# Three kinds of small elementwise work of a recurrent mixer moved from VectorE to GpSimd

## Chip, cores and metric

The kernel runs on one core of one Trainium2 chip. The metric is the device time of one execution in microseconds (us), as the median of three runs. The engines are named as in the profile: PE is TensorE, DVE is VectorE, ACT is ScalarE, POOL is GpSimd, SP is SyncE, which issues the transfers.

## What is computed

Two sequences of 512 tokens, each of width 1024, go through a trunk of two layers. Each layer projects the tokens, runs two token mixers beside each other, merges them with gates and ends with a squared-ReLU MLP. The mixer that matters here is a bidirectional gated linear recurrence with eight heads of 64 keys and 64 values:

```python
def step(S, inp):
    qc, kc, vc, gc = inp
    b = jnp.cumsum(gc, axis=2)
    diff = b[:, :, :, None, :] - b[:, :, None, :, :]
    dec = jnp.exp(jnp.where(tri[:, :, None], diff, -jnp.inf))
    A = jnp.einsum('bhtd,bhsd,bhtsd->bhts', qc, kc, dec)
    o = jnp.einsum('bhts,bhse->bhte', A, vc) + jnp.einsum('bhtd,bhde->bhte', qc * jnp.exp(b), S)
    ...
k_f, g_f = gates(hf_fwd, lower[0])
k_b, g_b = gates(hf_bwd, lower[1])
o_f = gla_chunk_scan(q, k_f, v, g_f)
o_b = rev(gla_chunk_scan(rev(q), rev(k_b), rev(v), rev(g_b)))
o = o_f + o_b
```

## The kernel before

Both sequences (the kernel calls them groups, g = 0 and 1) pass each layer together. All large products are done in three passes of rounded halves (`mm3`, L152 to L154, tile `mm`), and each weight block that comes in is split into such halves: ACT casts it (L131) and POOL, or in some places DVE, subtracts (L132, tile `w`).

The recurrent mixer is `hgrn`. It handles two heads at a time, so it has four passes p = 0 to 3 for each layer. The decay is not computed as a table of differences; the block of scores is built up over levels of distance h = 1, 2, 4 and so on to 64. At each level `grow` multiplies queries Q (L418) and keys K (L422) by products of the gates, and `tot` (L428) holds those products. For h = 2 to 64 the two heads' queries are laid out in a block-diagonal tile `bd`: `spread` copies the first head's 64 partitions with ACT (L348) and the second head's with DVE (L346). PE then multiplies (`quads`, L355, or L399 in `far`), and DVE writes the results into `near` under a mask (`keep`, L363). At level h = 32 (`middle`) the four 32-row quarters of `near` are copied into the score tile `at` (L390), beside the products of that level, which DVE and ACT take from PSUM in turn (L386). At h = 64 (`far`) ACT copies the results (L406).

The distance-one neighbours are done apart, in `pairs`, once for each pass and group. A straight product `ox` and a crosswise product `other` (L253: queries of even places by keys of odd ones and the other way round, two instructions of 128x256) are each split into halves (ACT L258, DVE L259), summed over a head's channels by PE (L261 and L262, each pair into one bank `sm`), and multiplied by the values (DVE L264 for `ox`, L267 for `other`); POOL adds the two (L270).

While PE runs pass p's levels, the projections of pass p + 1 (`prep`, whose instructions fill PE between the levels) run between them: `weave` takes one step of each in turn. In the last pass the gates' projections take their place. Pass 0's `prep` runs alone, ahead of everything, in each layer.

What sets the order: every engine runs its own instructions strictly in the order in which the program's scheduler put them, and waits at semaphores for the others. The scheduler places instructions by its own estimates, so a change of engine for some of them can also change the order of others. `pool_copy` (L134 and L135) is a helper that copies on POOL, as a multiplication by 1.0; before, it is used once, for the first weight block.

Of the kernel before, what the change touches and what calls it, by code (L numbers as in the profile page):

```python
# [87 lines left out]
def tile_encoder_trunk(  # L88
# [6 lines left out]
    nc = tc.nc  # L95
# [16 lines left out]
    def sm_ps():  # L112
        return psum.tile([P, 512], F32, tag="sm", name="sm")
# [20 lines left out]
    def pool_copy(dst, src):  # L134
        nc.gpsimd.tensor_scalar(dst, src, 1.0, None, op0=ALU.mult)  # L135
# [94 lines left out]
    def hgrn(l, x, gate):  # L230
        with tc.tile_pool(name=f"hg{l}", bufs=1) as hp:
# [14 lines left out]
            def t2k(dt=F32):  # L246
                return hp.tile([P, SEQ], dt, tag="t2k", name="t2k", bufs=4)

            def pairs(r, vt):
                ox = r["ox"]  # L250
                other = t2k()
                for i in range(2):
                    nc.vector.tensor_tensor(  # L253
                        other[:, i::2], r["q"][:, i, i::2], r["k"][:, 1 - i, 1 - i::2], op=ALU.mult
                    )
                hi, lo = t2k(F32R), t2k(F32R)
                for w in (ox, other):
                    nc.scalar.copy(hi, w)  # L258
                    nc.vector.tensor_tensor(lo, w, hi.bitcast(F32), op=ALU.subtract)  # L259
                    ps = sm_ps()  # L260
                    nc.tensor.matmul(ps, ones, hi, start=True, stop=False)  # L261
                    nc.tensor.matmul(ps, ones, lo, start=False, stop=True)  # L262
                    if w is ox:
                        nc.vector.scalar_tensor_tensor(ox, ps, 64.0, vt, op0=ALU.mult, op1=ALU.mult)  # L264
                        continue
                    for i in range(2):
                        nc.vector.scalar_tensor_tensor(  # L267
                            w[:, i::2], ps[:, i::2], 64.0, vt[:, 1 - i::2], op0=ALU.mult, op1=ALU.mult
                        )
                    nc.gpsimd.tensor_tensor(ox, ox, w, op=ALU.add)  # L270

            def prep(p, u):
                for col in (C_FF, C_FB, C_HQ, C_HI, C_HG):
# [7 lines left out]
                    for g in (range(NG), (1, 0))[l > 0 and p == 0]:  # L281
# [28 lines left out]
                        elif col == C_HI:  # L310
                            vt = t2k()
                            nc.scalar.copy(vt, ps)
                            ps = sm_ps()
                            for c in range(4):
                                s = slice(c * P, (c + 1) * P)
                                nc.tensor.transpose(ps[:, s], vt[:, s], ident)
                            v = hp.tile([P, 4, P], F32, tag="V", name="V", bufs=2)
                            nc.scalar.copy(v, ps)
                            r["v"] = v
                            pairs(r, vt)  # L320
                        else:
                            sg = t2k()
                            nc.scalar.activation(out=sg, in_=ps, func=AF.Sigmoid)
                            hg = hp.tile([P, SEQ], F32, tag="hg", name="hg", bufs=2)
                            nc.vector.tensor_tensor(hg, ps, sg, op=ALU.mult)
                            r["hg"] = hg
# [7 lines left out]
            def queries(r, h):  # L334
                return bass.AP(
                    r["q"].tensor, r["q"].offset, [list(r["q"].ap[0]), [2 * h, SEQ // (2 * h)], [SEQ + h, 2], [1, h]]
                )

            def spread(g, src):
                for e in range(2):  # L340
                    hs = slice(64 * e, 64 * e + 64)
                    dst = bd[g][hs, e, :]
                    if len(src.shape) == 4:
                        dst = dst.rearrange("p (n x h) -> p n x h", x=2, h=src.shape[3])
                    if e:
                        nc.vector.tensor_copy(dst, src[hs])  # L346
                    else:
                        nc.scalar.copy(dst, src[hs])  # L348

            def quads(g, lhs, swap):  # L350
                ps = sm_ps()
                for c in range(4):
                    for i in range(4):
                        o = c * P + 32 * (i ^ swap)
                        nc.tensor.matmul(  # L355
                            ps[32 * i:32 * i + 32, c * 64:(c + 1) * 64].rearrange("p (e t) -> p e t", e=2),
                            lhs(c, i), bd[g][:, :, o:o + 32], start=True, stop=True,
                            tile_position=(0, 32 * i),
                        )
                return ps  # L360
# [8 lines left out]
            def short(g, r, n, h):  # L369
                spread(g, queries(r, h))  # L370
                kx = hp.tile([P, SEQ], F32, tag="kx", name="kx", bufs=2)
                nc.scalar.copy(kx.rearrange("p (n x h) -> p n x h", x=2, h=h), keys(r, h))
                ps = quads(g, lambda c, i: kx[:, c * P + 32 * i:c * P + 32 * i + 32], 0)
                keep(g, ps, n)

            def middle(g, r):
                spread(g, queries(r, 32))
                ps = quads(
                    g, lambda c, i: r["k"][:, i % 2, c * P + 32 * i:c * P + 32 * i + 32], 1
                )  # L380
                A, N = at[g], near[g]
                for i in range(4):
                    hs = slice(32 * i, 32 * i + 32)
                    o = 32 * (i ^ 1)
                    eng = nc.scalar.copy if i % 2 else nc.vector.tensor_copy
                    eng(  # L386
                        A[hs, :, :, o:o + 32].rearrange("p c e t -> p (c e) t"),
                        ps[hs, :256].rearrange("p (c t) -> p c t", t=32),
                    )
                    nc.vector.tensor_copy(A[hs, :, :, hs], N[hs])  # L390

            def far(g, r):
                spread(g, queries(r, 64))
# [382 lines left out]
    for l in range(DEPTH):  # L776
# [9 lines left out]
        for k in (4, 5, 6, 7, 0, 1, 2, 3):  # L786
            raw = raw_tile()
            nc.sync.dma_start(raw, o_sp[l][k])
            for g in range(NG):
                src = raw[:, g * SEQ:(g + 1) * SEQ]  # L790
# [292 lines left out]
```

## Time and profile before

| | |
|---|---|
| median of three runs | 3065.37 us (3060.91 to 3068.12) |
| profiled execution, its own time | 3064.09 us |
| its span, first to last instruction | 3062.3 us |
| PE busy | 2956.7 us, 97% of the span |
| DVE busy | 1666.7 us, 54% |
| ACT busy | 1090.9 us, 36% |
| POOL busy | 865.8 us, 28% |
| the two recurrent mixers, in us of the span | about 55 to 395 and 1590 to 1910 |

Busy time is the time in which an engine ran an instruction. The chain of work that ended last goes through PE for 81% of the span and through DVE for 10%. A row of a timeline gives start, duration, engine, line, operation, tile written and tiles read, shapes and count, and in brackets how long the engine had stood idle and what ended that. A row of instructions of the same kind that follow each other has one start and one duration for all of them.

### The profile page before, as it was taken

How to read it: one execution, taken by the hardware profiler on the slowest of the kernel's cores; microseconds unless marked ns; L12 is line 12 of the kernel's file. 1: busy time of each engine (PE TensorE's matmuls, PEld its weight loads, DVE VectorE, ACT ScalarE, POOL GpSimd, SP SyncE). 2: the span in 40 equal slices, each digit the busy share in tenths (PEclk: the TensorE clock that was granted, in tenths of full speed). 3: DMA queues.
4: the chain of work that ended last, by engine and by line, in shares of the span. 5: the costliest groups of instructions: out<-in, count | busy, mean ns of one | idle time of the engine just before them, and what ended most of it. 6: DMA issues, size and time to landing. Idle time of an engine off the chain costs nothing.

```text
span 3062.3 us, 42748 instructions
## 1 busy us (share of the span) xinstructions
PE 2956.7 (97%) x16720; PEld 2399.4 (78%) x16720; DVE 1666.7 (54%) x2877; ACT 1090.9 (36%) x1826; POOL 865.8 (28%) x532
## 2 busy tenths in 40 slices
PE   8999999999999999999889999999999999999997
PEld 6777787877888887888667777878878888878885
DVE  5888748126543333445768887481265433344448
ACT  3344447323121112433434444473231211124333
POOL 4222120112222222454542221101231222234544
PEclk9999999999999999999999999999999999999999
DMA  3111232246123346533321112322460243564333
GB/s 127 36 42 36 67 89 69 80 162 218 34 86 134 132 167 241 169 97 97 113 75 36 42 36 69 90 64 100 157 226 9 93 144 125 177 255 144 97 97 107
DMA packets 278890, 331.98 MB, mean 108 GB/s; under 512 B 16545, under 2 KB 185121, under 8 KB 274593
## 3 DMA queue, kind: packets, MB, share of 16 engines
q1 hardware_dynamic: 276816, 325.00, 32.5%
q10 hardware_dynamic: 1872, 4.26, 0.4%
q8 instruction: 131, 2.15, 0.3%
q14 instruction: 71, 0.57, 0.1%
HBM read 230.38 MB, written 92.27 MB: 105 GB/s over the span
## 4 chain that ended last, share of the span: by engine, by line
PE 81%; DVE 10%; DMA 3%; issue 3%; POOL 1%; ACT 1%; SPq 0%; ACTq 0%; POOLq 0%; DVEq 0%
PE mm L152 17%; PE mm L154 16%; PE mm L153 16%; PE sm L971 3%; PE sm L972 3%; PE sm L973 3%; PE mm L972 3%; PE mm L971 3%; PE mm L973 3%; PE mm L864 2%; PE mm L866 2%; PE mm L865 2%; PE sm L695 1%; PE sm L641 1%; PE sm L685 1%
## 5 line engine op out<-in xcount | busy, mean ns | idle before, releaser
L152 PE MATMUL mm<-X,w 128*128 128x512 f32 x2624 | 1033.4, 394 | 4.8 <-ACT w L131 4.1
L153 PE MATMUL mm<-X,w 128*128 128x512 f32 x2624 | 1028.7, 392 | 0.0
L154 PE MATMUL mm<-X,w 128*128 128x512 f32 x2624 | 1026.2, 391 | 1.1 <-POOL w L132 1.1
L132 POOL TENSOR_TENSOR w<-raw,w 128x1024 fp32r<-128x1024 f32 (+1 forms) x179 | 417.9, 2336 | 1370.9 <-ACT w L131 1255.2
L152 PEld LDWEIGHTS mm<-X,w 128*128 128x128 f32 x2624 | 493.6, 188 | 111.8 <-ACT w L131 4.5
L154 PEld LDWEIGHTS mm<-X,w 128*128 128x128 f32 x2624 | 493.8, 188 | 102.3 <-POOL w L132 2.2
L153 PEld LDWEIGHTS mm<-X,w 128*128 128x128 f32 x2624 | 493.8, 188 | 98.6 <-DVE X L793 0.5
L131 ACT CAST w<-raw 128x1024 fp32r<-128x1024 f32 (+1 forms) x330 | 332.1, 1007 | 365.4 <-PE sm L973 106.7
L902 DVE TENSOR_TENSOR X<-t 128x512 f32<-128x512 f32 x128 | 88.6, 692 | 427.8 <-ACT t L901 427.8
L961 POOL TENSOR_TENSOR raw<-X 128x512 f32<-128x512 f32 x160 | 221.8, 1388 | 263.6 <-DVE w L132 259.4
L132 DVE TENSOR_TENSOR w<-raw,w 128x1024 fp32r<-128x1024 f32 x153 | 195.7, 1283 | 168.9 <-ACT w L131 168.7
L901 ACT ACTIVATE t<-mm 128x512 f32<-128x512 f32 x128 | 76.5, 598 | 554.7 <-PE mm L154 546.8
L971 PE MATMUL mm<-w 128*128 128x512 f32 x480 | 190.2, 397 | 11.3 <-ACT w L131 11.3
L972 PE MATMUL mm<-w 128*128 128x512 f32 x480 | 190.3, 396 | 3.7 <-DVE w L132 3.6
L973 PE MATMUL mm<-w 128*128 128x512 f32 x480 | 189.1, 394 | 0.0
L971 PE MATMUL sm<-w 128*128 128x512 f32 x384 | 149.5, 389 | 0.0
L973 PE MATMUL sm<-w 128*128 128x512 f32 x384 | 149.4, 389 | 0.0
L972 PE MATMUL sm<-w 128*128 128x512 f32 x384 | 149.4, 389 | 0.0
L793 DVE TENSOR_TENSOR X<-raw,X 128x512 fp32r<-128x512 f32 x32 | 20.8, 690 | 197.5 <-ACT X L792 197.4
L971 PEld LDWEIGHTS mm<-w 128*128 128x128 f32 x480 | 91.7, 191 | 32.0 <-ACT w L131 12.6
L864 PE MATMUL mm<-X 128*128 128x512 f32 x256 | 103.9, 406 | 11.2 <-DVE t L823 11.2
L959 POOL TENSOR_TENSOR w<-X,w 128x512 fp32r<-128x512 f32 x64 | 85.4, 1334 | 98.8 <-ACT w L955 98.6
(187 smaller groups left out, 3848.9 us busy)
## 6 DMA issues: line engine op xcount, KB each, us to landing
raw<-hsp SPq DMA_DIRECT2D x224, 256.0 KB
raw<-in_w_in_dram SPq DMA_DIRECT2D x84, 512.0 KB
raw<-in_w_ff_dram SPq DMA_DIRECT2D x64, 512.0 KB
hsp<-X SPq DMA_DIRECT2D x32, 1024.0 KB
X<-in_w_ff_dram SPq DMA_DIRECT2D x32, 1024.0 KB
gates<-gt SPq DMA_DIRECT2D x64, 256.0 KB
t<-gates SPq DMA_DIRECT2D x64, 256.0 KB
hsp<-X SPq DMA_DIRECT2D x32, 512.0 KB
```

Source lines behind the costliest of these rows:

```text
L131: (first or nc.scalar.copy)(hi, src)
L132: (eng or nc.gpsimd).tensor_tensor(lo, src, hi.bitcast(F32), op=ALU.subtract)
L152: nc.tensor.matmul(ps, ah, bh, start=(i == 0), stop=False)
L153: nc.tensor.matmul(ps, ah, bl, start=False, stop=False)
L154: nc.tensor.matmul(ps, al, bh, start=False, stop=(i == n - 1))
L864: nc.tensor.matmul(pend[j, n], mh, wh, start=(k == 0), stop=False)
L902: nc.vector.tensor_tensor(out[g], t, t, op=ALU.mult)
L959: nc.gpsimd.tensor_tensor(w[:, 1, 512:], src, w[:, 0, 512:].bitcast(F32), op=ALU.subtract)
L961: nc.gpsimd.tensor_tensor(raw[:, 512:], block(b0, k), block(b1, k), op=op)
L971: nc.tensor.matmul(ps[r], hh, wh, start=first, stop=False, **kw)
L972: nc.tensor.matmul(ps[r], hh, wl, start=False, stop=False, **kw)
L973: nc.tensor.matmul(ps[r], hl, wh, start=False, stop=stop, **kw)
```

## The change

```diff
             def pairs(r, vt):
                 ox = r["ox"]
                 other = t2k()
                 for i in range(2):
-                    nc.vector.tensor_tensor(
+                    nc.gpsimd.tensor_tensor(
                         other[:, i::2], r["q"][:, i, i::2], r["k"][:, 1 - i, 1 - i::2], op=ALU.mult
                     )
...
             def spread(g, src):
...
                     if e:
-                        nc.vector.tensor_copy(dst, src[hs])
+                        pool_copy(dst, src[hs])
                     else:
                         nc.scalar.copy(dst, src[hs])
...
             def middle(g, r):
...
-                    nc.vector.tensor_copy(A[hs, :, :, hs], N[hs])
+                    pool_copy(A[hs, :, :, hs], N[hs])
```

GpSimd makes the second head's spread queries (96 copies of 64x512), the copies of the near quarters (64 of 32x256) and the crosswise products (32 of 128x256). The scheduler also places other instructions anew. Three places follow; the numbers in names are buffers.

POOL from level h = 32 of the first pass to the crosswise products of the second, before. `w` are split weights, `K_751` the keys of the next pass.

```order
L295 TENSOR_SCALAR K_751<-F_750 128x512
L132 TENSOR_TENSOR w_1383<-raw_1381,w_1383 128x1024
L132 TENSOR_TENSOR w_1472<-raw_1470,w_1472 128x1024
L270 TENSOR_TENSOR ox_1011<-ox_1011,t2k_1187 128x512
L132 TENSOR_TENSOR w_1643<-raw_1641,w_1643 128x1024
L270 TENSOR_TENSOR ox_1109<-ox_1109,t2k_1316 128x512
```

The same stretch of POOL after the change.

```order
L295 TENSOR_SCALAR K_751<-F_750 128x512
L135 TENSOR_SCALAR bd0_247<-Q_414 64x512
L135 TENSOR_SCALAR at0_251<-near0_249 32x8x32 x4
L135 TENSOR_SCALAR bd1_248<-Q_448 64x512
L135 TENSOR_SCALAR at1_252<-near1_250 32x8x32 x4
L132 TENSOR_TENSOR w_1383<-raw_1381,w_1383 128x1024
L135 TENSOR_SCALAR bd0_247<-Q_414 64x512
L135 TENSOR_SCALAR bd1_248<-Q_448 64x512
L132 TENSOR_TENSOR w_1472<-raw_1470,w_1472 128x1024
L253 TENSOR_TENSOR t2k_1187<-Q_1009,K_668 128x256 x2
...
L253 TENSOR_TENSOR t2k_1316<-Q_1107,K_751 128x256 x2
L132 TENSOR_TENSOR w_1643<-raw_1641,w_1643 128x1024
```

The split of `w_1383` stands behind two spreads and eight copies, and each crosswise product behind a split.

DVE from the queries of the next pass (`Q_1107`, L304) to the first split of the straight product (L259), before.

```order
L304 TENSOR_TENSOR Q_1107<-t2k_1105,F_750 128x1024
L309 TENSOR_TENSOR ox_1109<-ox_1109,t2k_1105 128x512
L422 TENSOR_TENSOR K_289<-K_289,tot_1044 128x4x64
L422 TENSOR_TENSOR K_318<-K_318,tot_1076 128x4x64 x2
L428 TENSOR_TENSOR tot_1146<-tot_1076 128x8
L253 TENSOR_TENSOR t2k_1187<-Q_1009,K_668 128x256 x2
L422 TENSOR_TENSOR K_668<-K_668,F_667 128x256
L418 TENSOR_TENSOR Q_1009<-Q_1009,F_667 128x256x2
L259 TENSOR_TENSOR t2k_1191<-ox_1011,t2k_1190 128x512
```

After the change.

```order
L304 TENSOR_TENSOR Q_1107<-t2k_1105,F_750 128x1024
L309 TENSOR_TENSOR ox_1109<-ox_1109,t2k_1105 128x512
L422 TENSOR_TENSOR K_289<-K_289,tot_1044 128x4x64
L422 TENSOR_TENSOR K_318<-K_318,tot_1076 128x4x64 x2
L422 TENSOR_TENSOR K_668<-K_668,F_667 128x256
L418 TENSOR_TENSOR Q_1009<-Q_1009,F_667 128x256x2
L259 TENSOR_TENSOR t2k_1191<-ox_1011,t2k_1190 128x512
```

The crosswise products are gone from the row, but L422 writes the keys `K_668` that they read and so waits for POOL here; the rest keeps its order.

PE at the crosswise and straight products of the second pass's group 0, before: `sm_1180` are the transposed values, `sm_1194` the sums of the straight product.

```order
L316 MATMUL sm_1180<-ident_77,t2k_1178 128x128 x4
L261 MATMUL sm_1194<-t2k_1190,ones_244 128x512
L153 MATMUL mm_1282<-X_87,w_1150 128x512
L154 MATMUL mm_1282<-X_86,w_1150 128x512
L152 MATMUL mm_1282<-X_86,w_1150 128x512
L153 MATMUL mm_1282<-X_87,w_1150 128x512
L262 MATMUL sm_1194<-t2k_1191,ones_244 128x512
```

After the change.

```order
L316 MATMUL sm_1180<-ident_77,t2k_1178 128x128 x4
L261 MATMUL sm_1194<-t2k_1190,ones_244 128x512
L153 MATMUL mm_1282<-X_87,w_1150 128x512
L154 MATMUL mm_1282<-X_86,w_1150 128x512
L262 MATMUL sm_1194<-t2k_1191,ones_244 128x512
```

Two of the four large products that stood ahead of L262 now stand behind it. In group 1 the five that stood between L316 and L261 stand behind the `finish` products of the pass.

## Rows read from the trace of the kernel before

**Rows 1.** Stretches (mixers): length; busy us (instructions) of PE, PEld, DVE, ACT, POOL; clock; DMA

```profile
55.00:395.00 340.00, 326.39 (x2974) 255.98 (x2973) 275.07 (x577) 152.47 (x248) 70.73 (x42) 0.99 0.16 47
...
1590.00:1910.00 320.00, 306.39 (x2865) 240.65 (x2863) 267.85 (x558) 142.39 (x234) 78.42 (x52) 1.00 0.15 45
```

**Rows 2.** Waits of PE: line, waited for, total us, times, longest us

```profile
PE sm L262 <- DVE t2k L259: 17.1, 8, 2.7
...
PE sm L399 <- DVE bd L346: 10.1, 6, 1.8
```

**Rows 3.** The moved instructions by source line: ns min/median/max, first and last start

```profile
L253 DVE TENSOR_TENSOR t2k<-Q,K x32: 410/416/2566, 56.8 to 1836.2; 128x256 f32<-128x256 f32 x32
...
L346 DVE COPY bd<-Q x96: 424/425/2623, 59.8 to 1891.3; 64x512 f32<-64x512 f32 x96
...
L390 DVE COPY at<-near x64: 266/284/2391, 107.5 to 1886.7; 32x256 f32<-32x256 f32 x64
```

**Rows 4.** POOL's instructions of like kind, by source line

```profile
L295 POOL TENSOR_SCALAR K<-F x32: 620/634/1124, 25.9 to 1799.5; 128x512 f32<-128x512 f32 x32
...
L135 POOL TENSOR_SCALAR w<-raw x1: 2775/2775/2775, 12.8 to 12.8; 128x1024 fp32r<-128x1024 f32 x1
...
L270 POOL TENSOR_TENSOR ox<-ox,t2k x16: 1272/1384/1407, 62.9 to 1840.8; 128x512 f32<-128x512 f32 x16
```

**Rows 5.** Timeline of POOL and DVE at level h = 32, second pass

```profile
187.59 0.62 POOL L295 TENSOR_SCALAR K<-F 128x512 f32<-128x512 f32 x1 [6.07 <-ACT F L290]
188.58 2.39 POOL L132 TENSOR_TENSOR w<-raw,w 128x1024 fp32r<-128x1024 f32 x1 [0.37 <-ACT w L131]
...
188.88 3.14 DVE L390 COPY at<-near 32x256 f32<-32x256 f32 x4
...
196.58 1.20 DVE L304 TENSOR_TENSOR Q<-t2k,F 128x1024 f32<-128x1024 f32 x1
```

**Rows 6.** Timeline of DVE, ACT and POOL from level h = 64 to L259

```profile
201.61 0.60 ACT L298 ACTIVATE t2k<-mm 128x512 f32<-128x512 f32 x1
...
203.22 2.65 POOL L132 TENSOR_TENSOR w<-raw,w 128x1024 fp32r<-128x1024 f32 x1 [12.25 <-ACT w L131]
...
203.64 0.69 DVE L300 SCALAR_TENSOR_TENSOR t2k<-mm,t2k 128x512 f32<-128x512 f32 x1
204.25 1.90 DVE L422 TENSOR_TENSOR K<-K,tot 128x256 f32<-128x256 f32 x1
206.07 1.21 DVE L304 TENSOR_TENSOR Q<-t2k,F 128x1024 f32<-128x1024 f32 x1
...
210.84 0.69 DVE L259 TENSOR_TENSOR t2k<-ox,t2k 128x512 fp32r<-128x512 f32 x1
```

**Rows 7.** Timeline of PE in the same stretch

```profile
201.79 1.97 PE L399 MATMUL sm<-bd,K 128*64 128x128 f32 x32 [1.53 <-DVE bd L346]
...
211.72 0.39 PE L153 MATMUL mm<-X,w 128*128 128x512 f32 x1
211.94 0.39 PE L262 MATMUL sm<-t2k,ones 128*128 128x512 f32 x1
```

**Rows 8.** Timeline at group 1's crosswise products, second pass, of four engines

```profile
220.61 0.59 ACT L312 COPY t2k<-mm 128x512 f32<-128x512 f32 x1 [4.84 <-PE mm L154]
221.09 1.05 ACT L131 CAST w<-raw 128x1024 fp32r<-128x1024 f32 x1
...
222.28 2.38 POOL L132 TENSOR_TENSOR w<-raw,w 128x1024 fp32r<-128x1024 f32 x1 [5.90 <-ACT w L131]
...
222.37 2.90 DVE L253 TENSOR_TENSOR t2k<-Q,K 128x256 f32<-128x256 f32 x2
...
225.93 0.50 PE L262 MATMUL sm<-t2k,ones 128*128 128x512 f32 x1 [2.12 <-DVE t2k L259]
```

**Rows 9.** Timeline of PE at the wait of each layer's lone first prep

```profile
69.69 0.50 PE L262 MATMUL sm<-t2k,ones 128*128 128x512 f32 x1 [2.69 <-DVE t2k L259]
...
1600.91 0.50 PE L262 MATMUL sm<-t2k,ones 128*128 128x512 f32 x1 [1.88 <-DVE t2k L259]
```

## The prediction

> **What bounds the kernel now.** I read three views in this order. The busy time by stretch says where the change can act at all: in the two mixers PE is busy for 326.39 of 340 and 306.39 of 320 us [rows 1], so about 27 us, 0.9% of the time, are all that a faster partner could give back there. DVE is the engine closest behind it, 275.07 and 267.85 us, while POOL has 70.73 and 78.42. The waits of PE say what these 27 us are: L262 waits for DVE's L259 eight times, 17.1 us, and L399 for DVE's L346 six times, 10.1 us [rows 2]. Both are DVE work, and L346 is one of the moved lines. The timelines then show each wait's shape. It comes once a pass in passes whose fill is another pass's projections, plus once in each layer's first prep. Elsewhere in the mixers PE does not wait, so nothing that is moved can gain there, and slower copies there cost nothing while projections cover them.
>
> A row that matters for all the rest is how DVE and POOL disturb each other. Four copies L390 take 3.14 us where a POOL split runs [rows 5], against a median of 0.284 each [rows 3]. An L422 of 128x256 takes 1.90 beside the split at 203.22, where L253 of the same shape has a median of 0.416, while L300, which reads PSUM, has 0.69 there [rows 3, 6]. So some DVE instructions stand still until POOL's ends.
>
> **The change part by part.** Off DVE go 96 x 0.425 + 64 x 0.284 + 32 x 0.416 = 72 us by the medians of [rows 3]. Onto POOL come 96 copies of 64x512, 64 of 32x256, and 32 products of 128x256. POOL's nearest copy-like row is L295, 0.634 for 512 columns; I take it for the spread, and 0.35 for 256 columns. The other end is the one copy by this very helper, L135, 2.775 for 1024 columns [rows 4], which would mean 1.39 and 0.69. It is POOL's first arithmetic of the run and a single case, so I stay with L295 and keep L135 for the range. A crosswise product is half of L270's 1.384 plus a little: 0.73, against 0.416. POOL gets 61 + 22 + 23 = 107 us more in both mixers, where it has room. What counts is only how the waits move. I go through them with the new order.
>
> A. The far wait, six times, 10.1 us. Before, L346 stands behind all of DVE's L386 and L422, and PE waits 1.53 [rows 7]. Now the spread is on POOL: from 187.59 [rows 5] it runs L295, two spreads, eight copies and the split (2.39), 0.62 + 1.27 + 2.8 + 2.39 = 7.1, so to 194.7, then the two far spreads to 196. PE comes at 201.79 - 1.53 = 200.26. That leaves 4 us, which even three collisions with DVE instructions of 0.7 each don't use up. Next late are the keys (L422), which DVE writes shortly before L346 today; they no longer stand behind L390's 3.14. I count the whole -10.1, with a residue of 1 us each (6 in all) as the other end.
>
> B. The straight product of group 0, six times, no wait before. L259 ends at 210.84 + 0.69 = 211.53 and PE takes L262 at 211.94: 0.41 to spare [rows 6, 7]. Now PE comes 1.53 earlier by A, and two of the four large products that covered it stand behind it, 0.22 each by the starts in [rows 7]: it arrives at 209.95. When does L259 end? DVE's line there is tied to a chain: L386 lets ACT go on, ACT runs L298 at 201.61 and casts, POOL splits from 203.22, and the split holds up an L422 until 206.15; L304 follows [rows 6]. Without L390 and L346 DVE reaches L386 earlier, but L298 can't run before PE's products end at 200.26, so at most 1.3 are won; the split now sits behind the near copies and meets L304, so I take 0.9 (other end: 0.3 lost). Then the crosswise products leave DVE (2 x 0.416), but their POOL versions can't start before L304 has written Q, and L422 waits for them; next to L309 and the L422 they take turns with DVE, 2 x 0.73 = 1.46, net +0.6. So L259 ends at 211.53 - 0.9 + 0.6 = 211.25, and PE waits 1.3. Six times: +7.8. Ends: no wait if the two engines don't take turns (0), and 211.53 + 0.3 + 0.6 against 209.95, 2.5 (+15).
>
> C. Group 1, six times, 17.1 - 2.69 - 1.88 = 12.5 us [rows 2, 9]. Before, the cast L131 stands ahead of the straight product's own cast, the split begins at 222.28 and L253 stands still beside it until 225.27; L259 follows, PE waits 2.12 [rows 8]. Now L253 is done long before, on POOL, and the straight product's L259 passes. But the weight cast comes behind it, and the split then stands in front of the crosswise product's L259, with the same 2.4 us. Counting from the end of the projection: L312 0.6, L258 0.62, L131 1.05, so the split starts at about 2.6 and ends at 5.1, and L259 at 5.65; PE comes to its L262 at about 4.0 (four large products 0.9, transposes 0.6, then L261, two products, L262, two products, L261, two products, three products of the pass's end). A wait of 1.65 for 2.1: six times, -2.6. Ends: -12.5 if the split slips behind L259, +2.5 if DVE also takes a `tot` product first.
>
> D. The lone prep of each layer, 4.57 us [rows 9]. The same two mechanisms, without a far wait to gain: 1.05 for the first straight product (two cover products fewer, 0.45, and 0.6 for POOL's crosswise product), 1.05 and 1.65 for group 1. 3.75 twice is 7.5: +2.9. Ends: -4.6 and +5.
>
> What else moves: at the short levels the spreads gate PE's L355 and DVE's L418. There POOL needs L295 and two spreads, 1.9, and often the split, 2.4, in a period of 6.7 (level to level), all under 24 large products; they cost nothing unless POOL needs over 6 us. Transfers and SP's queue keep their order.
>
> The sum is -10.1 + 7.8 - 2.6 + 2.9 = -2.0 us. It is made on the profiled execution, 3064.1 with a span of 3062.3; the median lies 1.3 above that, so the forecast is 3065.4 - 2.0 = 3063.4.
>
> One rule bears on B and C. In the rows, L300 reads PSUM beside the split and is not slowed, while L422, with two tiles in SBUF, is [rows 6]. The Trainium skill (SBUF — State Buffer, section Who interferes with whom) says the same: a DVE instruction with two SBUF inputs, or a fast copy, excludes a GpSimd instruction that reads SBUF, for its whole length. If every moved microsecond on POOL were so paid back, 107 for 72, B to D would stand at their upper ends; the rows show that masked copies and PSUM readers fill part of DVE's line, so I don't count it so.
>
> **The rivals.** First, the waits simply go: DVE, 72 us lighter, reaches L259 in time, B and D's loss are 0, C as above: -10.1 - 2.6 = -12.7, 3052.7. It decides at B: L304 must start by 206.07 - (211.53 + 0.6 - 209.95) = 203.9. For it: DVE is the nearest engine and both waits are DVE's. Against: the chain through ACT and the split that sets L304. If all 27.2 went, 3038; I give that 0.02 within this.
>
> Second, slower: the near copies push the split of `w_1383` from 188.58 to 192.3 or later, and it then runs when DVE wants group 0's L304, at 196.58 today [rows 5]. From the point where L295 and POOL's ten copies take over 196.58 - 2.39 - 187.59 = 6.6 us, L304 stands still (its 1.2), and each pass's DVE line is that much later: B grows by 7.2 and A keeps 0.5 each, 3: 3063.4 + 10.2 = 3073.6. For it: POOL's 4.7 and three turns of 0.7 for DVE's L308 and two L418 reach the point. Against: those turns needn't all fall so.
>
> Third, slower: a POOL copy costs what L135 says. From 187.6: 0.62 + 2.78 + 5.5 + 2.39, to 198.9, far spreads at 200.3 and 201.7, waits of 0.8 stay in A (-5.3); DVE, which waits for the spreads in L418, is later, B 2.9 (+17.4); C -2.6, D +5: sum +14.5, 3079.9.
>
> That the change doesn't do what it says, DVE merely standing still while POOL does the work, is the Trainium skill's rule too (Perfetto Trace Analysis, section Optimizing Scalar/DVE Operations: moving work between these two may not help, since they share a port). In my rows that is B's taking turns, and it gives the forecast's own time, not a separate one.
>
> **How the numbers follow.** Forecast 0.45, first rival 0.25, second 0.18, third 0.12. About 0.2%, 6.1 us, is what a measurement of this kernel can tell from no change. The forecast's own spread of 6 or so lies mostly within it. Faster: 0.25 and a tail of 0.03 of the forecast, 0.28. Slower: 0.12, 0.14 of the second rival, 0.03 of the forecast, 0.29. Same: 0.43. The range, 3050 to 3080, goes from the first rival with a little more to the third's centre. The likeliest case's own range is 3057 to 3070.
>
> **What would show it.** A: L399 with no wait for `bd`. B: a new wait of L262 at group 0, about 1.3, six times, with L422 on DVE waiting for POOL's L253. C: group 1's wait moved from the first L262 to the second, behind a slowed L259. D: more than one wait of L262 in each lone prep. POOL's L135 near 0.63 and 0.35 tells the third rival off. Wrong it would be if L304 started before 203.9 in the second pass and yet L262 waited, or if PE began to wait in L355.

## The result, and the profile after

The changed kernel takes 3118.36 us (median of 4 runs, 3116.86 to 3118.95); the kernel before took 3066.11 on the same chip. The ratio is 1.0172, with a 95% interval of 1.0155 to 1.019. So it is 1.7% slower. The prediction said 3063.4 and a range of 3050 to 3080: it was wrong, and the time lies well outside the range. The profiled execution of the changed kernel has a span of 3116.1 us against 3062.3, 53.8 more, and the rest of this section and the next says where they are.

The stretches of the two mixers, which answer to [rows 1] and are longer now (columns: length; busy us and instructions of PE, PEld, DVE, ACT, POOL; granted clock; DMA share; GB/s):

```profile
55.00:415.00 360.00, 333.75 (x2958) 259.55 (x2957) 243.31 (x481) 152.73 (x247) 207.88 (x138) 0.97 0.15 44
1610.00:1960.00 350.00, 321.21 (x2860) 249.59 (x2859) 240.31 (x463) 144.96 (x236) 218.08 (x146) 0.96 0.14 42
```

DVE lost about 30 us in each, 59 together, where 72 had been counted. POOL gained some 140 us in each, where 107 had been counted for both together. The granted clock of the two stretches, 0.99 and 1.00 before, is 0.97 and 0.96.

The waits of PE, which answer to [rows 2] (line, waited for, total us, times, longest us):

```profile
PE sm L399 <- POOL bd L135: 22.4, 10, 3.7
PE sm L355 <- POOL bd L135: 19.1, 11, 3.2
...
PE sm L262 <- DVE t2k L259: 12.9, 12, 1.6
```

Together 54.4 us, against 17.1 + 10.1 = 27.2 before: 27.2 more. The far wait L399 did not go, it doubled, and it now waits for POOL. L355, which had no wait, has 19.1. Only L262 has less. PE's busy time over the whole span is 2984.2 us against 2956.7, for the same 16720 instructions: 27.5 more. These two halves make 54.7, within 1 us of the span's 53.8. The trace's record of the granted clock says what the second half is: in the mixers the clock fell to half behind twelve waits and took 25.6 us of full-speed work, against one fall and 1.7 us before; elsewhere it took 35.8 against 34.5.

The moved copies, by source line, which answer to [rows 3] and [rows 4] (duration in ns, min/median/max):

```profile
L135 POOL TENSOR_SCALAR bd<-Q x96: 1487/1542/2181, 60.0 to 1940.5; 64x512 f32<-64x512 f32 x96
...
L135 POOL TENSOR_SCALAR at<-near x64: 842/848/2602, 110.4 to 1935.5; 32x256 f32<-32x256 f32 x64
```

A spread costs at least 1.49 us and a near copy 0.84. I had taken 0.634 and 0.35, from L295, and had kept 1.39 and 0.69, from the one copy by this helper, "for the range".

What that does in the second pass: first POOL's timeline, then PE's (start, us, engine, line; in brackets the wait before it):

```profile
194.38 0.62 POOL L295 TENSOR_SCALAR K<-F 128x512 f32<-128x512 f32 x1 [2.25 <-ACT F L290]
195.09 2.00 POOL L135 TENSOR_SCALAR bd<-Q 64x512 f32<-64x512 f32 x1
197.16 4.09 POOL L135 TENSOR_SCALAR at<-near 32x256 f32<-32x256 f32 x4
201.34 1.49 POOL L135 TENSOR_SCALAR bd<-Q 64x512 f32<-64x512 f32 x1
202.91 5.92 POOL L135 TENSOR_SCALAR at<-near 32x256 f32<-32x256 f32 x4
208.91 2.35 POOL L132 TENSOR_TENSOR w<-raw,w 128x1024 fp32r<-128x1024 f32 x1
211.35 3.56 POOL L135 TENSOR_SCALAR bd<-Q 64x512 f32<-64x512 f32 x2
```

```profile
202.88 0.65 PE L355 MATMUL sm<-bd,K 128*32 128x64 f32 x32 [2.00 <-POOL bd L135]
...
212.90 4.05 PE L399 MATMUL sm<-bd,K 128*64 128x128 f32 x32 [3.70 <-POOL bd L135]
```

POOL works without a break from 194.38 to 214.9. The near copies of group 0 stand in front of group 1's middle spread, so L355 waits 2.00; the near copies of group 1 and the split stand in front of the far spreads, so L399 waits 3.70. The last line shows the second half of the loss as well: the 32 products of L399 take 4.05 us, where they took 1.97 before [rows 7]. Around the wait, in stretches of 4 us (columns as above):

```profile
202.88:206.88 4.00, 4.00 (x47) 3.34 (x48) 3.94 (x7) 1.17 (x3) 3.91 (x2) 1.00 0.01 4
...
212.90:216.90 4.00, 3.90 (x33) 3.17 (x33) 3.11 (x4) 1.16 (x2) 3.90 (x2) 0.50 0.37 110
216.90:220.90 4.00, 4.00 (x17) 3.31 (x16) 3.97 (x5) 1.16 (x2) 2.76 (x3) 0.84 0.45 130
```

Behind the wait of 2.00 us the granted clock is 1.00 (2.4 GHz); behind the one of 3.70 it is 0.50, the lower level of 1.2 GHz, over 4 us, and in part of the next 4. So this long wait was paid twice: once as the wait, and once as slower products.

### The profile page after: what moved, and what is told of

It is laid out like the page before. It is cut to its first block, busy times and chain, and to the rows that moved or that the text cites. A ratio compares the mean times of both kernels' runs of the same rounds, so it can differ in the third digit from the quotient of the medians.

```text
span 3116.1 us, 42844 instructions
## 1 busy us (share of the span) xinstructions
PE 2984.2 (96%) x16720; PEld 2417.1 (78%) x16720; DVE 1602.7 (51%) x2685; ACT 1092.4 (35%) x1826; POOL 1143.7 (37%) x724
## 3 DMA queue, kind: packets, MB, share of 16 engines
q8 instruction: 131, 2.15, 0.3%
## 4 chain that ended last, share of the span: by engine, by line
PE 79%; DVE 7%; POOL 6%; issue 3%; DMA 2%; ACT 2%; SPq 0%; POOLq 0%; ACTq 0%; DVEq 0%
PE mm L152 16%; PE mm L153 16%; PE mm L154 16%; PE mm L972 3%; PE mm L971 3%; PE sm L971 3%; PE sm L972 3%; PE mm L973 3%; PE sm L973 3%; POOL bd L135 2%; PE mm L864 2%; PE mm L866 2%; PE mm L865 2%; PE sm L695 1%; POOL at L135 1%
## 5 line engine op out<-in xcount | busy, mean ns | idle before, releaser
L132 POOL TENSOR_TENSOR w<-raw,w 128x1024 fp32r<-128x1024 f32 (+1 forms) x179 | 426.6, 2384 | 1224.3 <-ACT w L131 1134.7
L135 POOL TENSOR_SCALAR bd<-Q 64x512 f32<-64x512 f32 x96 | 160.7, 1674 | 82.5 <-DVE Q L418 33.0
L418 DVE TENSOR_TENSOR Q<-Q,tot 128x512 f32<-128x512 f32 x96 | 71.1, 741 | 110.0 <-POOL bd L135 99.7
```

Source lines behind the costliest of these rows:

```text
L132: (eng or nc.gpsimd).tensor_tensor(lo, src, hi.bitcast(F32), op=ALU.subtract)
```

## The experiments

Two theories stood first. P: POOL's copy in this form is dear, the row of copies comes late, and the clock falls behind the waits. W: POOL is slow on few partitions, or DVE and POOL stand still for one another, whatever the copy's form. In the table each run's ratio is to the kernel before on the same chip; "waits" is the total of PE's waits at L262, L355, L399 and L478 in us, "PE" its busy time over the profiled execution. A profiled execution is one run of several, and its busy time carries some 5 us of chance: outside the mixers, where the kernels hardly differ, the granted clock's falls took between 34.1 and 39.3 us in the fourteen profiles, and 34.5 in that of the kernel before. So a difference of a few us in the last column is no finding by itself.

| kernel | median us | ratio (95%) | waits | PE busy |
|---|---|---|---|---|
| before (profile) | 3063.7 to 3067.1 | 1 | 27.2 | 2956.7 |
| changed | 3118.36 | 1.0172 (1.0155 to 1.019) | 54.4 | 2984.2 |
| change, copy with two operations | 3077.55 | 1.0030 (1.0016 to 1.0044) | 28.8 | 2968.6 |
| change, plain copy (one run) | 3073.2 | | 27.5 | 2964.2 |
| change without the crosswise part | 3122.67 | 1.0192 (1.0178 to 1.0206) | 57.3 | 2983.9 |
| near copies alone | 3078.96 | 1.0034 (1.0021 to 1.0047) | 31.7 | 2964.9 |
| spreads alone | 3073.9 | 1.0024 (1.0015 to 1.0034) | 28.3 | 2966.1 |
| crosswise alone | 3070.71 | 1.0007 (0.9997 to 1.0017) | 27.8 | 2964.8 |
| spreads alone, two operations | 3064.29 | 0.9996 (0.9988 to 1.0005) | 22.0 | 2962.6 |
| spreads and near, two operations | 3068.05 | 1.0005 (0.9996 to 1.0014) | 23.1 | 2965.8 |
| spreads, crosswise of group 1, two operations | 3066.23 | 1.0007 (0.9998 to 1.0016) | 22.4 | 2965.4 |
| before, far wait lengthened | 3091.87 | 1.0080 (1.0065 to 1.0095) | 44.3 | 2971.7 |
| spreads, two operations, two splits on DVE | 3056.6 | 0.9969 (0.9956 to 0.9981) | 14.1 | 2963.7 |
| before, two splits on DVE | 3054.93 | 0.9963 (0.9949 to 0.9977) | 18.6 | 2960.0 |

**The price of the copy.** The changed kernel, with only the helper edited:

```diff
     def pool_copy(dst, src):
-        nc.gpsimd.tensor_scalar(dst, src, 1.0, None, op0=ALU.mult)
+        nc.gpsimd.tensor_scalar(dst, src, 1.0, 0.0, op0=ALU.mult, op1=ALU.add)
```

> The changed kernel with one thing edited: GpSimd's copy multiplies by 1.0 and then adds 0.0, so that its instruction has the two operations of L295 (0.62 us for 128x512) in place of one. Theory P, the price: the one-operation copy is dear (1.49 and 0.84 us against my 0.634 and 0.35), POOL's row of two spreads and eight copies behind L295 is therefore late, PE waits in L355 and L399, and the granted clock falls after these waits. By P the copies now take about 0.63 and 0.35, PE waits for bd under 3 us in all instead of 41.5, PE's busy time in the two mixers goes back to about 633 us, and the time is what I forecast, 3063, give or take 8. Rival W, the place: POOL is slow with copies that reach only 64 or 32 partitions, or DVE and POOL stand still for one another, whatever the operation; then the copies keep 1.4 and 0.8 us and the time stays within 10 us of 3118.

The same copies now, by source line:

```profile
L135 POOL TENSOR_SCALAR bd<-Q x96: 616/669/1303, 58.6 to 1900.7; 64x512 f32<-64x512 f32 x96
...
L135 POOL TENSOR_SCALAR at<-near x64: 395/403/2277, 109.3 to 1897.0; 32x256 f32<-32x256 f32 x64
...
L135 POOL TENSOR_SCALAR w<-raw x1: 1045/1045/1045, 12.6 to 12.6; 128x1024 fp32r<-128x1024 f32 x1
```

With one operation more the instruction takes less than half the time: 0.62 for 1.49, 0.40 for 0.84, and the first weight's copy 1.05 for 2.78. W falls on this point: the partitions and the neighbours are the same. PE waits for `bd` only three times, under 1 us in all, and by the ratios some 43 of the 52 us are gone. It doesn't fall to 3063, nor into theory P's 8 us around it: 9 us remain (below). The helper's one older use, the copy of the first weight, is cheaper by the same edit (1.05 instead of 2.78): the mixers' first L261 begins at 56.9 us instead of 58.0, so about 1 us of what the two-operation form brings comes from there.

The third form, a plain copy in the same helper, has one run:

```diff
-        nc.gpsimd.tensor_scalar(dst, src, 1.0, None, op0=ALU.mult)
+        nc.gpsimd.tensor_copy(dst, src)
```

> The changed kernel with GpSimd's copy written as a plain copy instruction in place of the multiplication by 1.0. It asks only for the price of a third form beside the 1.49 and 0.84 us of the one-operation form and the 0.62 and 0.40 us of the two-operation form (64x512 and 32x256). Theory P (the price follows the form): anything between, and the time follows it: 3078 if it is as cheap as the two-operation form, 3118 if it is as dear as the other. Rival: one operation is dear because it is one; then a plain copy is at least 1.4 and 0.8 and the time is 3110 to 3125.

```profile
L135 POOL COPY bd<-Q x96: 608/659/1493, 58.7 to 1895.3; 64x512 f32<-64x512 f32 x96
...
L135 POOL COPY at<-near x64: 386/398/923, 109.3 to 1891.7; 32x256 f32<-32x256 f32 x64
```

It costs what two operations cost. Dear is only the multiplication alone, and not because it is a single operation.

**Each part alone**, in the form of the change, put into the kernel before: the near copies (L390), the spreads (L346), the crosswise products (L253).

```diff
-                    nc.vector.tensor_copy(A[hs, :, :, hs], N[hs])
+                    pool_copy(A[hs, :, :, hs], N[hs])
```

> The kernel before with one part of the change, the copies of the near quarters on GpSimd (one operation, L390). Theory P: 8 x 0.84 = 6.7 us of POOL behind L295 in each pass, with no spread in the row that PE waits for; DVE loses 2.3 us of work, and 12.6 where it stood beside a split; the split of the next weight slips by 6.7 and meets the fill of the projections that it feeds only after 30 large products. So 0 to -6 us: 3060 to 3066. Rival W: POOL's copies and DVE's instructions stand still for one another; the eight copies cost DVE more than they took from it, L346 and L304 come later, and the waits of PE at L399 and L262 grow by 1 to 2 us in each of six passes: 3072 to 3078.

```diff
-                        nc.vector.tensor_copy(dst, src[hs])
+                        pool_copy(dst, src[hs])
```

> The kernel before with one part of the change, the second head's spread queries on GpSimd (one operation, L346), 96 copies of 1.49 us. Theory P, by the queue: the two far spreads now stand behind L295, the two middle spreads and one split, 0.62 + 3.0 + 2.4, and end well before PE comes for them, so the six waits of L399 (10.1 us) go; at the short levels two spreads of 1.49 plus a split of 2.4 stay under the 24 large products between levels. A wait of L355 at the middle level of up to 2 us stays in six passes. Together 3058 to 3068. Rival: the spread copy by itself is too slow for its level (it ends 1.1 us later than DVE's 0.42 would), and PE waits at L355 in most of the levels of each pass: 3080 or more.

```diff
-                    nc.vector.tensor_tensor(
+                    nc.gpsimd.tensor_tensor(
                         other[:, i::2], r["q"][:, i, i::2], r["k"][:, 1 - i, 1 - i::2], op=ALU.mult
```

> The kernel before with one part of the change, the crosswise products on GpSimd (L253), 32 of 0.86 us. My terms B to D say: the straight product of group 0 stays where it was or is 0.5 later (no new wait, since PE comes no earlier than before), the wait of group 1 goes from the first L262 to the second and shrinks from 2.1 to about 1.6 (-2.6), and the two lone preps lose 2.9 us together: 3064 to 3068. Rival: the crosswise products lengthen DVE's line by as much as they last on POOL, and L262 waits in more places than twelve: 3072 or more.

They cost 10, 7 and 2 us (by the ratios), the last not to be told from nothing; none of the three times lies in the range of its theory. With the near copies alone, theory P's 0 to -6 was wrong: DVE's far spread came later, the wait of L399 grew to 2.36 and 2.53, and the clock fell behind six waits of the mixers instead of one. With the spreads alone the far wait went in the first layer and came back in the second, behind DVE's keys. The two rows, from the near copies alone and from the spreads alone:

```profile
PE sm L399 <- DVE bd L346: 14.7, 6, 2.5
```

```profile
PE sm L399 <- DVE K L422: 7.2, 3, 2.4
```

Why DVE's far spread came later, in the second pass: first two keys' products in the kernel before, then the same two with the near copies alone, and POOL's split there.

```profile
198.87 0.76 DVE L422 TENSOR_TENSOR K<-K,tot 128x256 f32<-128x256 f32 x2
```

```profile
199.39 3.00 DVE L422 TENSOR_TENSOR K<-K,tot 128x256 f32<-128x256 f32 x2
199.71 2.40 POOL L132 TENSOR_TENSOR w<-raw,w 128x1024 fp32r<-128x1024 f32 x1
```

The split slipped behind eight dear copies and met L422. So W's standing still has a part in this loss, though beside the split and not beside the copies.

The crosswise part did in group 1 what term C said, and more: the wait is 0.89 there, where C had 1.65. The two lone preps lose 4.5 us by it, not the 2.9 of term D. The sum of the three, about 20, is not the 52 of the change. The next run says why.

**The row of copies.** The changed kernel, with the crosswise products back on DVE:

```diff
-                    nc.gpsimd.tensor_tensor(
+                    nc.vector.tensor_tensor(
```

> The changed kernel with the crosswise products back on DVE: the spreads and the near copies on GpSimd, in the one-operation form. Apart they cost 7 and 10 us. Theory P says that their sum is not what counts: only together do they make the row of two spreads and eight copies (3.0 + 6.7 us behind L295) that PE catches up with, so waits at L355 and L399 of 2.0 to 3.7 each pass, the clock down behind them, and nearly all of the loss: 3105 to 3118. Rival: the parts add, 3080 to 3086, and the rest of the change's loss needs the crosswise products.

```profile
PE sm L399 <- POOL bd L135: 24.3, 13, 3.7
PE sm L355 <- POOL bd L135: 18.9, 11, 3.2
```

It has the whole loss, 59 us by its ratio. Each kind of copy alone leaves POOL time to catch up; both together are the row from 194.38 on that is shown above. The crosswise part has no share in the loss of the change; its ratio lies 0.002 above that of the change, with intervals that overlap.

**The clock.** The kernel before, where DVE makes group 0's far spread four times instead of once; nothing moves between the engines. (Lines from 347 on are one higher in this kernel: its L400 is L399.)

```diff
-                        nc.vector.tensor_copy(dst, src[hs])
+                        for _ in range(4 if g == 0 and len(src.shape) == 4 and src.shape[3] == 64 else 1):
+                            nc.vector.tensor_copy(dst, src[hs])
```

> The kernel before with one thing added: DVE makes the far level's spread copy of group 0 four times over instead of once, so that PE's six waits of 1.5 and 1.8 us at L399 grow by 3 x 0.42 = 1.27 us each, to 2.8 and 3.1. Nothing else is moved. Theory K, the clock: after a wait of that length the granted clock falls to about half for some 4 us, as it did after the 2.53 us of the run with the near copies alone (0.57 over 4 us there, about 1.7 us lost): 7.6 us of longer waits and 6 x 1.5 to 2 us of slower products, 3082 to 3087. Rival, waits only: 3073 to 3075, and PE's busy time as before.

```profile
PE sm L400 <- DVE bd L347: 27.2, 8, 4.3
```

```profile
216.61 3.55 PE L400 MATMUL sm<-bd,K 128*64 128x128 f32 x32 [4.00 <-DVE bd L347]
```

```profile
216.61:220.61 4.00, 4.00 (x34) 3.75 (x35) 1.84 (x6) 1.55 (x3) 0.00 (x0) 0.59 0.07 22
```

The waits grew more than I meant, to 4.0 and 4.3, because other DVE work (L300, L304, L309) came between the copies and one copy stood 1.78 us beside a split; so the time lies above theory K's range as well. In all the waits grew by 17.1 us. The profiled execution's span grew by 31.6, and 15.0 of it is PE's busy time. By the record of the clock, its falls in the mixers took 17.1 us against 1.7 before: 12.0 behind the six lengthened waits, 2.0 each, with the clock at 0.59 over the 4 us behind the one shown, and 5.1 behind three waits at L262 (2.68, 2.12 and 1.88). Theory K's mechanism holds: waits alone would have left the busy time as it was.

How long must a wait be? Over the fourteen profiles (before, after, twelve experiments) I set each of PE's waits of 0.8 us or more in the mixers (50 to 400 and 1590 to 1910 us) beside the granted clock of the 4 us behind it. Of 95 waits under 1.75 us, 3 were followed by a clock under 0.95, and these three stood right behind another wait. Of 88 from 1.75 to 2.2 it was 30, of 18 from 2.3 to 2.75 it was 11, and of 19 over 3 us all. The waits of the kernel before, 1.5 to 2.1 us but for one of 2.69, lie where the fall begins; in its profile one of 14 was followed by it.

**What is left with a cheap copy.** Put together from the edits above: the kernel before with the spreads alone on POOL in the two-operation form, and the same with the near copies added, the crosswise products on DVE in both.

> The kernel before with the spread queries alone on GpSimd, in the two-operation form (0.62 us each). With the one-operation form the six waits of L399 went in layer 0 but came back behind DVE's L422 in layer 1 (2.41), and L262 at group 0 had a new 1.05. With the price off, the keys should not be held up: L399 waits for nothing in either layer (-10.1), L262 at group 0 keeps about 1.0 (+6), group 1's 2.07 stays, and the first L262 of each layer keeps its gain (-3). No wait over 2.1, so no fall of the clock: 3057 to 3062. Rival: DVE's keys L422 still end last in layer 1, by collisions with the split; the wait of L399 stays there, with clock lost behind it: 3068 to 3075.

> The kernel before with the spread queries and the copies of the near quarters on GpSimd, both in the two-operation form, and the crosswise products left on DVE. It is the first experiment without the crosswise part. If the crosswise part makes the 2.15 at group 0's L262 (there DVE's L422 and L309 take turns with it), this wait falls to about 1.0 and group 1's goes back to 2.07; with L399 at 0 to 0.3 that gives 6 x (1.0 + 2.07) + 2 = 20 us of waits against 27.2 before and no clock lost: 3058 to 3064. Rival: the wait at group 0 has its cause in the split that slips behind the near copies and meets L304; then it stays at 2.0 or more, with clock lost behind it: 3070 to 3080.

L399's wait is gone in both layers (or 0.28), as A had said, and L262 waits 1.05 at group 0. The waits are 22.0 and 23.1 instead of 27.2, but the time is the same within the interval, in both cases between the range of the first theory and that of its rival: behind group 1's unchanged 2.07 the clock fell after three of six in the first of these profiles, and after two of six in the second, 5.1 and 3.4 us against 1.7 before. The near copies add nothing, for or against. From the second of these kernels to the full change with the cheap copy, which differs by the crosswise part alone, the ratio rises from 1.0005 to 1.0030, some 8 us: they belong to the crosswise part. What it does is seen at group 0. DVE there, in that kernel (the change with two operations), with the split and the two products on POOL:

```profile
205.64 2.40 POOL L132 TENSOR_TENSOR w<-raw,w 128x1024 fp32r<-128x1024 f32 x1 [3.18 <-ACT w L131]
207.99 2.84 POOL L253 TENSOR_TENSOR t2k<-Q,K 128x256 f32<-128x256 f32 x2
```

```profile
205.06 0.69 DVE L300 SCALAR_TENSOR_TENSOR t2k<-mm,t2k 128x512 f32<-128x512 f32 x1
205.66 2.65 DVE L422 TENSOR_TENSOR K<-K,tot 128x256 f32<-128x256 f32 x1
208.24 1.88 DVE L304 TENSOR_TENSOR Q<-t2k,F 128x1024 f32<-128x1024 f32 x1
210.04 1.34 DVE L309 TENSOR_TENSOR ox<-ox,t2k 128x512 f32<-128x512 f32 x1
...
213.59 0.66 DVE L259 TENSOR_TENSOR t2k<-ox,t2k 128x512 fp32r<-128x512 f32 x1
```

L304 takes 1.88 beside POOL's products instead of 1.21 and L309 1.34 instead of some 0.67; DVE saved 0.83 by giving the products away and lost 1.34 beside them. And L422 stands 2.65 beside the split, where it stood 1.90 before [rows 6]: DVE, lighter, is through with L300 as the split begins, and meets all of it. PE waits 2.17 here, and in the second layer the clock fell behind all three of these waits.

I then gave POOL only the crosswise products of group 1, where they had helped:

```diff
-            def pairs(r, vt):
+            def pairs(r, vt, cross):
...
-                    nc.vector.tensor_tensor(
+                    cross.tensor_tensor(
...
-                            pairs(r, vt)
+                            pairs(r, vt, (nc.vector, nc.gpsimd)[r is u[1]])
```

> The kernel before with the spread queries on GpSimd in the two-operation form and, of the crosswise products, only those of group 1; those of group 0 and the near quarters stay on DVE. Each piece was seen apart: the spreads took L399's wait away and left 1.05 at group 0 and 2.07 at group 1; the crosswise products made group 1's wait 0.90 and group 0's 2.15. If the pieces add, a pass keeps 1.05 + 0.90, six times 11.7, with about 4 to 6 in the two lone preps: 16 to 18 us against 27.2 before. All these waits are below 1.9 us, after which no run so far shows the clock fall in the mixers at L262, so PE's busy time in the mixers should lose nothing to it either: 3050 to 3058, faster than before. Rival: group 1's products on POOL push the split or L270 later and meet group 0's chain of the next pass, and a new wait of 1 to 2 us per pass comes elsewhere: 3062 to 3070.

This failed. The wait moved once more, to L478, which the profile shows waiting for DVE's L264, and L264 stands behind an L428 that the split holds for 2.88. Nor was it right that no fall had followed a wait of 1.9 or less at L262: one of 1.88 had been followed by a clock of 0.57 with the near copies alone. Here the clock fell behind three waits, of 1.76 to 1.83.

```profile
PE sm L478 <- DVE ox L264: 10.9, 6, 1.8
```

```profile
223.87 2.59 POOL L132 TENSOR_TENSOR w<-raw,w 128x1024 fp32r<-128x1024 f32 x1 [4.70 <-ACT w L131]
```

```profile
224.13 2.88 DVE L428 TENSOR_TENSOR tot<-F 128x512 f32<-128x512 f32 x1
```

What DVE had in that place, L253 before, L259 in the change and L428 here, stood still beside the split each time (2.90, 2.15 and 2.88 us). The wait belongs to the split, it seems; the next runs test it.

**Taking the collision away.** So in the last two runs the split of one weight, that of the backward forget gate for the third and fourth pass, went the other way, from POOL to DVE: once in the kernel with the cheap spreads, once in the kernel before with nothing else.

```diff
-                            *((nc.vector.tensor_copy, nc.vector) if l == 0 and p == 0 and col in (C_FB,) else ()),
+                            *((nc.vector.tensor_copy, nc.vector) if l == 0 and p == 0 and col in (C_FB,) else (None, nc.vector) if p > 1 and col == C_FB else ()),
```

> The kernel with the spread queries on GpSimd in the two-operation form, and besides the rounding rest (split) of the backward forget weight of the third and fourth pass of each layer on DVE instead of POOL. In that kernel group 1's wait of 2.07 comes from this split: DVE's L253 at 221.78 stood 2.53 us beside it, against 0.42 alone. With the split in DVE's own line behind the norm's products, L253 has nothing to stand beside. Theory S (the wait is the collision with the split): four of the six waits of 2.07 go or fall below 0.5, minus 6 to 8 us, and with them their falls of the clock: 3050 to 3060. Rival: the DVE split of 1.26 us itself comes late, and the projection of that weight, or L325 and L488 behind it, makes a new wait of about the same size: 3062 to 3070.

> The kernel before with nothing changed but the split of the backward forget weight of the third and fourth pass of each layer on DVE; spreads, near copies and crosswise products stay on DVE. It tells whether group 1's wait needs any of the change to go. Theory S: four of the six waits of 2.1 us at L262 go or fall below 0.5, while the six waits of L399 (1.5 and 1.8) and the other two of L262 stay: minus 6 to 8 us, 3056 to 3060. Rival: DVE, which is the fuller engine here, hands the 1.26 us on, and the waits of L399 or a new one at the weight's projection take the place: 3062 to 3070.

Waits of PE in the second of them, and DVE at group 1's products in its second pass, which answers to [rows 8]:

```profile
PE sm L399 <- DVE bd L346: 9.9, 6, 1.8
PE sm L262 <- DVE t2k L259: 8.7, 4, 2.7
```

```profile
221.21 0.76 DVE L253 TENSOR_TENSOR t2k<-Q,K 128x256 f32<-128x256 f32 x2
221.89 0.68 DVE L259 TENSOR_TENSOR t2k<-ox,t2k 128x512 fp32r<-128x512 f32 x1
```

The two L253 take 0.76 us, where they took 2.90 [rows 8]; four of the six waits are gone, as theory S said, and the time is by the ratio 0.37% under that of the kernel before, 3054.93 against 3067.05, 1 us below theory S's range. Both kernels are faster than the kernel before with their whole intervals. The one that also has the spreads on POOL, with 4.5 us less of waiting, is not faster still: 3056.6, with intervals that overlap. Its profile shows two falls of the clock in the mixers and the other's three, but 39.3 us lost to the clock elsewhere against 34.1; two single profiles can't say why, and it stays open. That DVE can be relieved by POOL, the idea of the change, is not what helped; taking POOL's work out of DVE's way did. The Trainium skill (SBUF — State Buffer, section Who interferes with whom) states a rule that fits: a DVE instruction with two SBUF inputs contends with a GpSimd instruction that reads SBUF, for a pair of ports under an exclusive lock, and the order of issue decides who stands. The rows agree: L253, L422 and L428 stood 1.9 to 3.0 us beside splits of 2.4 to 2.7, and L300, which reads PSUM, took its 0.69.

## Why the prediction was wrong, step by step

- **The price of POOL's copy** is the step that failed, "POOL's nearest copy-like row is L295". The nearer row was L135, the same helper and the same instruction, and I set it aside as a single case. 1.49 and 0.84 were measured against 0.634 and 0.35. The difference makes 96 x 0.86 + 64 x 0.49 = 114 us on POOL, with some more for collisions: its busy time over the span rose by 277.9 us, not by 107. The far spreads did not end 4 us before PE came, as the sum had it; in the change PE came first and waited 2.3 to 3.7 us.
- **A**, L399's wait of 10.1 us gone: in the change it became 22.4. With a cheap copy the step holds, about 1 us or nothing was left. Its logic was right and its price was not.
- **"At the short levels ... they cost nothing unless POOL needs over 6 us"**: the condition came true at the middle level, where two spreads and eight copies took POOL from 195.09 to 208.9. L355 waits 19.1 us; my list had this as a way to be wrong.
- **B**, a new wait of 1.3 at group 0: not in the change, since PE comes later there by L399's wait. With the cheap copy it is 2.14 to 2.18, under the upper end of 2.5. The 0.6 for POOL's products was about right (1.34 - 0.83 = 0.5). Wrong was the 0.9 that DVE should win by being lighter: it met all of the split instead of part of it and lost 0.75.
- **C**: the place was right, the second L262 behind a slowed L259 (2.15 in the change). It was 0.90 us instead of 1.65, so -7 instead of -2.6.
- **D**: the lone preps wait 1.24 + 1.04 + 1.30 and 1.24 + 1.05 + 1.60, 7.5 us against 4.6: the +2.9 of the sum.
- **The clock** was in no step. In the change it made most of the second half of the loss: of the 27.5 us more of PE's busy time, 23.9 are falls in the mixers, beside 27.2 us more of waits. The sum treated a microsecond of waiting as a microsecond of time, which the rows at hand didn't contradict, since nearly all waits before lay under 2.2 us and the clock stood at 0.99 and 1.00 [rows 1].
- **The third rival** had the right mechanism, near the right price (1.39 and 0.69), and gave 3079.9. It left 0.8 us in the far wait where 2.3 to 3.7 came, because it let no collision lengthen the row (a spread of 2.00 at 195.09, four near copies in 5.92 instead of 3.4 at 202.91), and it knew neither L355's waits nor the clock. So even it, and the range drawn to its centre, ended 38 us short.

Open remains why the clock fell behind some waits of 2.07 us and not behind others of the same length and place, and so why the runs with 22 us of waits are no faster than the kernel before with 27. The falls differ in number between profiles, inside the mixers and outside them, but a single profile can't say how many a mean run has.

## What to carry to other kernels

Price a moved operation by the row of the very same instruction form, even if there is only one such row, and where two rows differ by a factor of two, work the whole sum out at both. Where PE runs nearly without a break, a wait of some 2 to 4 us costs more than its length, because the clock may fall behind it; a wait under 1.7 us cost its length here, unless it stood right behind another. Before work is moved from DVE to POOL, look at whether DVE's late instructions stand still beside POOL's: here less on POOL helped, and more didn't.

## What the runs showed of the hardware

- On POOL, a multiplication of fp32 by a constant as the only operation took 1.49 us for 64x512, 0.84 for 32x256 and 2.78 for 128x1024; with an addition of 0.0 behind it 0.62, 0.40 and 1.05, and as a plain copy 0.61, 0.39 and 1.04.
- These times go with the columns, not with the partitions: L295 takes 0.62 for 128x512, the spread 0.62 for 64x512.
- Behind a wait of over 3 us in the mixers the granted clock always fell to its lower level, and the 32 products of L399, where they stood behind such a wait, took 2.85 to 4.05 us instead of 1.97 (the lowest in the kernel with the lengthened far wait).
- Beside a split of 2.4 to 2.7 us on POOL, one or two of DVE's products of two SBUF tiles took 1.9 to 3.0 us (0.4 to 0.8 otherwise), while L300, which reads PSUM, took 0.69.
